# A gated DeltaNet layer step: the samples' gate column turned on VectorE and stored as rows, blocks of 8 spread through GpSimd's queue, the samples' substitution one block later

## The chip, the cores and the metric

The kernel runs on one core of a Trainium2 chip. The metric is the device time of one execution in microseconds (us). Before the change the median of three runs is 1664.96 us (1664.11 to 1667.59).

## The reference, cut to what matters

One decoder layer works on 256 prompt tokens and on 8 samples of 4 tokens each. One wide projection feeds a short gated convolution (A) and a gated DeltaNet mixer (B) of 8 heads; merge gates, an output projection, a layer norm, a feed-forward part and a second layer norm follow. The part that this document is about is the delta rule of mixer B:

```python
gcum = jnp.cumsum(gc, axis=-1)
diff = gcum[..., :, None] - gcum[..., None, :]
decay = jnp.where(causal, jnp.exp(jnp.where(causal, diff, 0.0)), 0.0)
M = jnp.where(strict, jnp.einsum('nbhid,nbhjd->nbhij', kb, kc) * decay, 0.0)
T = lax.linalg.triangular_solve(eye + M, eye, left_side=True, lower=True, unit_diagonal=True)
u = T @ (vc * bc)
w = T @ (kb * jnp.exp(gcum)[..., None])
```

For a pair of positions the decay is the difference of two running sums of the gate, so the kernel needs these sums both down the partitions (a column) and along the free axis (a row that every partition holds). The triangular matrix is inverted by forward substitution: the prompt's in blocks of 8 that are then merged to 16, 32 and 64, the samples' in blocks of 4.

## The kernel before, in words

All weights stream once from HBM in chunks of 512 KB (tile `raw`), which the text calls blocks, by their number. Float32 products are made of three matmuls, so each chunk is split: ScalarE copies it to a rounded high half (`hi`, L185), VectorE subtracts to make the low half (`lo`, L140, called from `split_lo`), and TensorE multiplies high by both halves of the activations (L217) and low by the high one (L219). A block has 24 such matmuls. The main loop (L1647 on) writes out the order by hand. In turn i it issues, in this order: the high split of block i + 3; one step of the side work; the low split of block i + 3; evacuations of finished accumulators that are due; the matmuls of block i; the load of block i + 7 on SP's queue. Each of the tiles `raw`, `hi` and `lo` has four buffers. So a load on SP waits until VectorE has made the low half that frees its buffer, and the splits are at most three blocks ahead of TensorE.

The side work is a Python generator: each `yield` ends the turn's step. It computes the gates (`gates`, L1019), then the delta rule for heads 0 to 3 (`gdn(0)`, called group 0) and 4 to 7 (group 1). Within each engine and each queue, instructions go in program order: a DMA on SP that waits for something holds every later weight load, and a VectorE instruction that waits holds the next low split.

What the change and the prediction's steps touch:

- L1083 to L1097: running sums by matmul; the prompt's sums are written to DRAM (`sums_d`) as rows from 16 partitions.
- L1113 to L1122: `s1` holds the samples' values per partition: column [.., 0, n] is the running sum of the gate, for the head groups n = 0, 1. L1121 writes each of the two columns to DRAM (`srow_d`), 128 single floats each.
- L1133, one turn later: SP reads them back as a row that is copied to all 128 partitions (`srow`); its reader is `sample()` (L1429), far on.
- L1212, one turn later again: SP reads the prompt's sums as rows into `gl`; VectorE's first use is E (L1234), three turns on.
- L1276 to L1283: VectorE makes the 8 x 8 diagonal blocks `n8`; SP writes them to DRAM (`eight_d`, L1279), and a turn later reads them back so that each partition holds its whole block (`X`, in tile `xt`, L1282). GpSimd's copies `move_sums(1)` stand between. Three turns on, VectorE starts the substitution (L1336 to L1344); its result goes to the matmuls of `pairs` (L1333).
- L1294: GpSimd's queue loads two of the group's four old states (L1146); later `spread_kq` on GpSimd (L1316); both are read by `states_of` (L1324).
- `sample()` is stepped from the same main loop after the side step. It writes 4 x 4 blocks to DRAM (L1439), reads them a turn later (L1441), moves k in quarters over two turns (`quarters`), then makes the substitution of 4 on VectorE (L1444 to L1450). A turn later its matmul follows (L1454).

Of the kernel before, what the change touches and what calls it, by code (L numbers as in the profile page):

```python
# [9 lines left out]
F32 = mybir.dt.float32  # L10
# [6 lines left out]
P = 128  # L17
# [85 lines left out]
def hybrid_kernel(ctx: ExitStack, tc: tile.TileContext, A):  # L103
# [3 lines left out]
    def pool(name, bufs=1, **kw):  # L107
        return ctx.enter_context(tc.tile_pool(name=name, bufs=bufs, **kw))

    cp = pool("cp")  # L110
# [5 lines left out]
    dp = pool("dp", space=bass.MemoryType.DRAM)  # L116
# [3 lines left out]
    def nm(s):  # L120
        counter[0] += 1
        return f"{s}{counter[0]}"

    def gtile():
        n = nm("g")
        return gp.tile([P, 512], F32, tag="g", name=n)
# [5 lines left out]
    def bmid(ap, n):  # L132
        sh = list(ap.shape)
        return ap.unsqueeze(1).to_broadcast([sh[0], n] + sh[1:])

    act, dve, pe, gps, sp = nc.scalar, nc.vector, nc.tensor, nc.gpsimd, nc.sync


    def tt(out, a, b, op):
        dve.tensor_tensor(out=out, in0=a, in1=b, op=op)  # L140
# [93 lines left out]
    def cst(n):  # L234
        a, b = CF_AT[n]
        if a >= NL:
            return ph["late"][:, a - NL:b - NL]
        return cf[:, a:b] if a < NE else cfe[:, a - NE:b - NE]
# [15 lines left out]
    epsc = cp.tile([P, 3], F32, name="epsc")  # L254
    hmr = cp.tile([P, P], F32R, name="hmr")
    sums_d = dp.tile([4, 2, 256], F32, name="sums_d")
    srow_d = dp.tile([2, P, 1], F32, name="srow_d")
    four_d = [dp.tile([32, 4, 4], F32, name=f"four_d{G}") for G in range(2)]
    eight_d = [dp.tile([16, 8, 64], F32, name=f"eight_d{G}") for G in range(2)]
    stBA = cp.tile([P, 32, 32], F32, name="stBA")  # L260
# [756 lines left out]
    G_ = {}  # L1017

    def gates(first):  # L1019
# [47 lines left out]
        tt(gm, bmid(g[:, 2, :], 8), bc(cst("bm3"), 8), MUL)  # L1067
        by_row = cp.tile([P, P], F32, name="by_row")
        gps.memset(by_row, 0.0)
        for r in range(2):  # L1070
            gps.tensor_copy(by_row[:, 8 * r:8 * r + 8].rearrange("p (n a b) -> p n a b", n=2, a=2),
                            g[:, 0:2, :].rearrange("p b (n r a) -> p r n a b", n=2, r=2)[:, r])
# [8 lines left out]
        q = gtile()  # L1081
# [29 lines left out]
        yield  # L1111
        next(first)
        s4 = cp.tile([P, 4, 8], F32, name="s4")  # L1113
        s1 = cp.tile([P, 4, 2], F32, name="s1")
        tt(s4[:, 0:2], q[:, 128:144].rearrange("p (q h) -> p q h", h=8), bmid(cst("sel"), 2), MUL)
        tt(s4[:, 2:4], sb, bmid(cst("sel"), 2), MUL)
        dve.tensor_reduce(out=s1.rearrange("p a b -> p (a b)"), in_=s4.rearrange("p q (g h) -> p (q g) h", h=4),
                          axis=mybir.AxisListType.X, op=ADD)
        sx = cp.tile([P, 4, 2], F32, name="sx")
        for n in range(2):  # L1120
            sp.dma_start(srow_d[n], s1[:, 0, n:n + 1])  # L1121
        act.activation(sx[:, 0:2, :], s1[:, 0:2, :], AF.Exp)  # L1122
        yield
        next(first)
# [4 lines left out]
                  egls=ge[:, 32:96].rearrange("p (b h) -> p b h", b=8),  # L1129
                  s_g=s1[:, 3, :], s_beta=s1[:, 2, :], s_eg=sx[:, 0, :], s_kd=sx[:, 1, :],  # L1130
                  s_neg=sx[:, 2, :], s_ngc=sx[:, 3, :])
        srow = cp.tile([P, 2, P], F32, name="srow")
        sp.dma_start(srow, srow_d.rearrange("n p o -> (o n) p").unsqueeze(0).to_broadcast([P, 2, P]))  # L1133
        G_["s_row"] = srow
        yield


    def gdn(G):
# [9 lines left out]
        def T(shape, tag):  # L1148
            return pl.tile(shape, F32, tag=tag, name=nm(tag))
# [8 lines left out]
        sqr = T([P, 1024], "vmh")  # L1158
# [34 lines left out]
        def move_k(copy, a, b):  # L1193
            for i in range(4):
                copy(kdec[64 * a + 32 * b:64 * a + 32 * b + 32, :, :, 32 * i:32 * i + 32],
                     ktv[32 * i:32 * i + 32, a, a, b])

        def move_sums(s):
            for b in range(2):
                for i in range(4):  # L1200
                    gps.tensor_copy(red4[64 * s + 32 * b:64 * s + 32 * b + 32, i].rearrange("p (c r) -> p c r", r=2),
                                    ptv[32 * i:32 * i + 32, 1 - s, b])
# [12 lines left out]
        total(3)  # L1215
        move_k(gps.tensor_copy, 0, 0)
        yield
        move_k(act.copy, 0, 1)
        yield
        sp2 = gtile()  # L1220
# [10 lines left out]
        X, Tm = xt[:, 0], xt[:, 1]  # L1231
# [35 lines left out]
        for u, q4, par, r in halves:  # L1267
# [8 lines left out]
        dve.tensor_reduce(out=n8, in_=Tm.rearrange("p q (b j) -> p q j b", b=8), axis=mybir.AxisListType.X, op=ADD)  # L1276
        tt(n8, n8, bmid(cst("i8u"), 8), MUL)
        tt(n8, n8, bmid(i8, 8), ADD)
        sp.dma_start(eight_d[G].rearrange("b k x -> (b k) x"), sqr[:, 0:64])  # L1279
        move_sums(1)  # L1280
        yield
        sp.dma_start(X.rearrange("p q c -> p (q c)"),  # L1282
                     eight_d[G].rearrange("b k x -> b (k x)").unsqueeze(1).to_broadcast([16, 8, 512]))  # L1283
        nb = X.rearrange("p q c -> p (q c)").rearrange("p (k q j) -> p q k j", k=8, q=8)
        kso = T([P, 2, P], "kso")
        kraw, ktok = (sqr[:, 512 + 256 * u:768 + 256 * u] for u in range(2))
# [121 lines left out]
        def quarters(out, src, side_):  # L1408

            act.copy(hl[:, 0], src)  # L1410
            tt(hl[:, 1], src, hl[:, 0], SUB)
            for hh in range(4):
                for w in range(4):
                    low = w // 2 if side_ == 0 else w % 2
                    d, r = out[32 * w:32 * w + 32, hh], hl[32 * hh:32 * hh + 32, low]
                    if side_ and w % 2:
                        act.copy(d, r)
                    else:
                        gps.tensor_copy(d, r)
                if hh % 2:  # L1420
                    yield

        def sample():

            sp1 = gtile()
            pe.matmul(sp1[:, 0:128], kst, kst, start=True, stop=True)
            pe.matmul(sp1[:, 128:256], kst, qst, start=True, stop=True)
            pe.transpose(sp1[:, 384:512], vfs.rearrange("p h b t -> p (h b t)"), ident)
            stt(Es, G_["s_row"][:, G], G_["s_ngc"][:, G:G + 1], cst("mbias4"), ADD, ADD)  # L1429
            act.activation(Es, Es, AF.Exp)  # L1430
            act.mul(vs, sp1[:, 384:512], snk)
            act.mul(kr, kr, sc[:, 0:1])
            stt(nMs, sp1[:, 0:128], sc[:, 2:3], Es, MUL, MUL)
            stt(aTs, sp1[:, 128:256], srk, Es, MUL, MUL)
            n4, u4, t4, r4 = (Ts[:, 4 * u:4 * u + (16 if u == 3 else 4)] for u in range(4))
            dve.tensor_reduce(out=n4, in_=nMs.rearrange("p (b j) -> p j b", j=4), axis=mybir.AxisListType.X, op=ADD)
            tt(n4, n4, cst("i4u"), MUL)
            tt(n4, n4, cst("i4"), ADD)
            sp.dma_start(four_d[G].rearrange("b k j -> (b k) j"), n4)  # L1439
            yield  # L1440
            sp.dma_start(r4, four_d[G].rearrange("b k j -> b (k j)").unsqueeze(1).to_broadcast([32, 4, 16]))  # L1441
            yield from quarters(kr3, kr, 0)
            rows4 = r4.rearrange("p (k j) -> p k j", k=4)
            dve.tensor_copy(u4, cst("i4"))  # L1444
            for j in range(1, 4):
                tt(t4[:, 0:j + 1], u4[:, 0:j + 1], rows4[:, 0:j + 1, j], MUL)
                dve.tensor_reduce(out=u4[:, j:j + 1], in_=t4[:, 0:j + 1], axis=mybir.AxisListType.X, op=ADD)
            tt(Us.rearrange("p (b j) -> p b j", j=4), u4.unsqueeze(1).to_broadcast([P, 32, 4]),
               cst("l4").rearrange("p (b j) -> p b j", j=4), MUL)
            stt(vs, kso[:, 0, :], G_["s_neg"][:, G:G + 1], vs, MUL, ADD)  # L1450
            act.mul(osm, kso[:, 1, :], G_["s_eg"][:, G:G + 1])
            yield
            pv_ = gtile()
            pe.matmul(pv_[:, 0:P], Us, vs, start=True, stop=True)  # L1454
            act.mul(vns, pv_[:, 0:P], sc[:, 1:2])
            v3 = pl.tile([P, 4, P], F32R, tag="U", name=nm("v3"))
            yield from quarters(v3, vns, 1)
            yield
            po = gtile()
            pe.matmul(po[:, 0:P], aTs, vns, start=True, stop=True)  # L1460
            tt(osm, osm, po[:, 0:P], ADD)
            done.append(1)
            vm = {}


            def spread(hh):
                if hh < 4:
                    vm[hh] = pl.tile([P, 8, P], F32R, tag=("vmh", "vml")[hh % 2], name=nm("vm"))
                    for b in range(8):
                        act.mul(vm[hh][:, b], v3[:, hh].bitcast(F32), cst("bmask")[:, b:b + 1])  # L1470

            spread(0)
            yield
            for hh in range(4):
                spread(hh + 1)
                if hh:
                    store(hh - 1)
                for j in range(2):
                    yield
                    pn = gtile()  # L1480
                    pe.matmul(pn, kr3[:, hh], vm[hh][:, 4 * j:4 * j + 4, :], start=True, stop=True)
                    for u in range(4):
                        b = 4 * j + u
                        stt(S0[:, hh, b], S0[:, hh, b], G_["egls"][:, b, 4 * G + hh:4 * G + hh + 1],
                            pn[:, u * P:u * P + P], MUL, ADD)
            yield
            store(3)
# [9 lines left out]
        o = T([P, 4, 2, P], "xt")  # L1497
# [103 lines left out]
    t, h0, l0 = raw.pop(0), his[0], los[0]  # L1601
# [170 lines left out]
```

## Time and profile before

| what | value |
|---|---|
| median of three runs | 1664.96 us |
| the profiled execution | 1664.45 us |
| its span, from first to last instruction | 1662.5 us |
| mean granted clock of TensorE | 0.999 |
| VectorE, ScalarE, GpSimd busy | 59%, 47%, 8% |
| mean DMA rate | 169 GB/s |

The profile is of one execution. Its span is shorter than the time by what lies around it, here 1.95 us. Rows of a timeline read: start, duration (us), engine, line, operation, out<-in, shapes, count, and in brackets the idle time of that engine just before and what ended it. SPq is a DMA that is issued on SP's queue; its duration is that of the issue, not of the transfer. In a list of waits the numbers are: us in total, times, longest. In a table by stretches of time they are: the stretch, its length, busy time and count of TensorE's matmuls, of its weight loads, of VectorE, ScalarE and GpSimd, then the granted clock, the DMA engines' mean busy share and GB/s.

### The profile page before, as it was taken

Reading aid. Unit: us, or ns where it says so; the run is one execution under the profiler, and the core shown is the slowest. Engines: PE = TensorE matmul, PEld = TensorE weight load, DVE = VectorE, ACT = ScalarE, POOL = GpSimd, SP = SyncE. Lnnn points to the kernel's source line nnn. Section 1 sums busy time; section 2 is a strip of 40 time slices with the busy share of each in tenths; the row PEclk is TensorE's granted clock in tenths of the full one; section 3 lists DMA queues with packets and bytes.
Section 4 is the critical chain, followed back from the end, with each engine's and each line's share of the span. In section 5 each row is a group of like instructions: output and inputs, shape, how many; then the busy total and the mean of one; then the engine's idle time right before and its main releaser. Section 6 shows DMA issues by size and latency. Waiting matters only on the chain.

```text
span 1662.5 us, 31404 instructions
## 1 busy us (share of the span) xinstructions
PE 1648.4 (99%) x13112; PEld 1633.2 (98%) x13112; DVE 977.4 (59%) x1305; ACT 782.6 (47%) x1224; POOL 134.9 (8%) x276
## 2 busy tenths in 40 slices
PE   9999999999999999999999999999999999999998
PEld 8989999999999999999999999999999999999998
DVE  6778677767544444457776666444444444444466
ACT  6776756457533333334444445443334433344344
POOL 1131315233000000000000000000000000000011
PEclk9999999999999999999999999999999999999999
DMA  8566466645755555555565555555555555555652
GB/s 263 167 165 183 138 186 194 195 117 152 213 165 166 165 163 169 167 166 164 159 219 165 164 168 162 167 165 166 167 164 165 165 167 167 165 165 165 181 162 100
DMA packets 275129, 281.40 MB, mean 169 GB/s; under 512 B 15108, under 2 KB 268601, under 8 KB 274725
## 3 DMA queue, kind: packets, MB, share of 16 engines
q1 hardware_dynamic: 271226, 267.31, 53.6%
q0 software_dynamic: 3616, 12.02, 2.5%
q8 instruction: 103, 1.69, 0.4%
q14 instruction: 40, 0.32, 0.1%
q10 hardware_dynamic: 144, 0.07, 0.0%
HBM read 271.79 MB, written 7.56 MB: 168 GB/s over the span
## 4 chain that ended last, share of the span: by engine, by line
PE 93%; DVE 2%; ACT 2%; DMA 2%; issue 1%; SPq 0%; ACTq 0%; DVEq 0%
PE acc L217 60%; PE acc L219 30%; DMA raw<-in_w_in_dram 1%; DVE lo L140 1%; PE acc L741 1%; ACT hi L185 1%; DMA srow_d<-s 1%; DVE w L143 0%; PE g L1333 0%; PE g L1503 0%; PE g L1523 0%; PE g L1526 0%; DMA xr<-in_x_prompt_dram 0%; PE g L1324 0%; PE g L1515 0%
## 5 line engine op out<-in xcount | busy, mean ns | idle before, releaser
L140 DVE TENSOR_TENSOR lo<-raw,hi 128x1024 fp32r<-128x1024 f32 (+1 forms) x503 | 606.8, 1210 | 577.5 <-ACT hi L185 576.5
L185 ACT CAST hi<-raw 128x1024 fp32r<-128x1024 f32 (+1 forms) x499 | 518.6, 1042 | 736.3 <-PE acc L217 643.0
L217 PE MATMUL acc<-xh,hi 128*128 128x288 f32 x1408 | 398.5, 299 | 0.5 <-ACT xh L948 0.4
L217 PE MATMUL acc<-xl,hi 128*128 128x288 f32 x1408 | 394.4, 295 | 0.0
L219 PE MATMUL acc<-xh,lo 128*128 128x288 f32 x1408 | 303.1, 296 | 5.4 <-DVE lo L140 5.3
L217 PE MATMUL acc<-dl,hi 128*128 128x288 f32 (+1 forms) x1024 | 287.7, 295 | 0.0
L217 PE MATMUL acc<-dh,hi 128*128 128x288 f32 (+1 forms) x1024 | 287.4, 295 | 0.0
L217 PE MATMUL acc<-hl,hi 128*128 128x288 f32 x992 | 277.8, 295 | 0.0
L217 PE MATMUL acc<-hh,hi 128*128 128x288 f32 x992 | 277.4, 294 | 0.0
L217 PEld LDWEIGHTS acc<-xh,hi 128*128 128x128 f32 x1408 | 265.0, 188 | 3.2 <-issue 1.6
L217 PEld LDWEIGHTS acc<-xl,hi 128*128 128x128 f32 x1408 | 264.8, 188 | 0.7
L219 PEld LDWEIGHTS acc<-xh,lo 128*128 128x128 f32 x1408 | 226.5, 188 | 6.9 <-DVE lo L140 6.9
L219 PE MATMUL acc<-dh,lo 128*128 128x288 f32 (+1 forms) x1024 | 219.7, 296 | 0.0
L219 PE MATMUL acc<-hh,lo 128*128 128x288 f32 x992 | 213.2, 296 | 0.0
L217 PEld LDWEIGHTS acc<-dh,hi 128*128 128x128 f32 x1024 | 193.3, 189 | 0.0
L217 PEld LDWEIGHTS acc<-dl,hi 128*128 128x128 f32 x1024 | 192.8, 188 | 0.0
L217 PEld LDWEIGHTS acc<-hh,hi 128*128 128x128 f32 x992 | 186.4, 188 | 0.4 <-issue 0.4
L217 PEld LDWEIGHTS acc<-hl,hi 128*128 128x128 f32 x992 | 186.1, 188 | 0.0
L219 PEld LDWEIGHTS acc<-dh,lo 128*128 128x128 f32 x1024 | 164.6, 188 | 0.0
L219 PEld LDWEIGHTS acc<-hh,lo 128*128 128x128 f32 x992 | 159.1, 188 | 0.0
L217 PE MATMUL acc<-mh,hi 128*128 128x288 f32 x256 | 71.9, 297 | 0.0
L217 PE MATMUL acc<-ml,hi 128*128 128x288 f32 x256 | 71.7, 295 | 0.0
(411 smaller groups left out, 1471.3 us busy)
## 6 DMA issues: line engine op xcount, KB each, us to landing
raw<-in_w_in_dram SPq DMA_DIRECT2D x175, 512.0 KB, 3.9
raw<-in_w_up_dram SPq DMA_DIRECT2D x128, 512.0 KB, 3.7
raw<-in_w_down_dram SPq DMA_DIRECT2D x128, 512.0 KB, 3.6
raw<-in_w_o_dram SPq DMA_DIRECT2D x32, 512.0 KB, 4.1
raw<-in_w_a_out_dram SPq DMA_DIRECT2D x16, 512.0 KB, 3.6
raw<-in_w_b_out_dram SPq DMA_DIRECT2D x16, 512.0 KB, 3.6
S<-in_state_gdn_dram POOLq DMA_DIRECT2D x8, 512.0 KB, 5.9
out_dram<-S POOLq DMA_DIRECT2D x8, 512.0 KB, 5.2
```

The lines of the kernel that those rows point to most:

```text
L140: dve.tensor_tensor(out=out, in0=a, in1=b, op=op)
L185: act.copy(his[i][:, k:k + step], raw[i][:, k:k + step])
L217: pe.matmul(o, h[:, k, c], x, start=st and x is xh_, stop=False)
L219: pe.matmul(o, l[:, k, c], xh_, start=False, stop=en)
L741: pe.matmul(out, x[:, kk, c], w[:, k, :], start=False, stop=stop)
```

## The change

The two columns are no longer written as single floats. `s1` becomes a part of a zeroed tile `st2`; one turn later VectorE transposes it in blocks of 32 x 32, so that each group of 32 partitions holds the sums of head groups 0 and 1 in its first two partitions as rows of 32 floats; SP writes four pieces of two such rows. The read-back moves from the gates into `gdn(0)`, three turns later than before, behind the read of `gl`. The write and the read of the blocks of 8 go from SP's to GpSimd's queue, and the read is issued in the turn of the write. In `sample()` one more `yield` stands before the substitution of 4; what follows in `sample()` comes a turn later too.

```diff
-    srow_d = dp.tile([2, P, 1], F32, name="srow_d")
+    srow_d = dp.tile([2, 4, 32], F32, name="srow_d")
...
         gps.memset(by_row, 0.0)
+        st2 = cp.tile([P, 2, 32], F32, name="st2")
+        gps.memset(st2, 0.0)
...
-        s1 = cp.tile([P, 4, 2], F32, name="s1")
+        s1 = st2[:, 0, 0:8].rearrange("p (a b) -> p a b", b=2)
...
         sx = cp.tile([P, 4, 2], F32, name="sx")
-        for n in range(2):
-            sp.dma_start(srow_d[n], s1[:, 0, n:n + 1])
         act.activation(sx[:, 0:2, :], s1[:, 0:2, :], AF.Exp)
         yield
...
-        srow = cp.tile([P, 2, P], F32, name="srow")
-        sp.dma_start(srow, srow_d.rearrange("n p o -> (o n) p").unsqueeze(0).to_broadcast([P, 2, P]))
-        G_["s_row"] = srow
+        dve.transpose(out=st2[:, 1], in_=st2[:, 0])
+        for n in range(4):
+            sp.dma_start(srow_d[:, n], st2[32 * n:32 * n + 2, 1])
+        G_["s_row"] = cp.tile([P, 2, P], F32, name="srow")
         yield
...
         move_k(gps.tensor_copy, 0, 0)
         yield
+        if G == 0:
+            sp.dma_start(G_["s_row"], srow_d.rearrange("n b t -> n (b t)").unsqueeze(0).to_broadcast([P, 2, P]))
         move_k(act.copy, 0, 1)
...
-        sp.dma_start(eight_d[G].rearrange("b k x -> (b k) x"), sqr[:, 0:64])
+        gps.dma_start(eight_d[G].rearrange("b k x -> (b k) x"), sqr[:, 0:64])
         move_sums(1)
-        yield
-        sp.dma_start(X.rearrange("p q c -> p (q c)"),
-                     eight_d[G].rearrange("b k x -> b (k x)").unsqueeze(1).to_broadcast([16, 8, 512]))
+        gps.dma_start(X.rearrange("p q c -> p (q c)"),
+                      eight_d[G].rearrange("b k x -> b (k x)").unsqueeze(1).to_broadcast([16, 8, 512]))
+        yield
...
             yield from quarters(kr3, kr, 0)
+            yield
             rows4 = r4.rearrange("p (k j) -> p k j", k=4)
```

## The prediction

> **What bounds the kernel now.** First the page: how busy TensorE is in the span.
>
> ```profile
> span 1662.5 us, 31404 instructions
> PE 1648.4 (99%) x13112; PEld 1633.2 (98%) x13112; DVE 977.4 (59%) x1305; ACT 782.6 (47%) x1224; POOL 134.9 (8%) x276
> ```
>
> TensorE works all the time; only 14.1 us of its span are idle, and only what an edit takes from this idle time can be won. Next the waits of TensorE, of which these three lie in the part that the diff touches (the others are at start and end):
>
> ```profile
> PE acc L219 <- DVE lo L140: 5.3, 4, 1.8
> PE g L1454 <- DVE b L143: 0.6, 1, 0.6
> PE g L1333 <- DVE U L1344: 0.2, 1, 0.2
> ```
>
> So 6.2 us is the most that can go. The timeline of TensorE between 107 and 131 us shows where the four waits of 5.3 us are:
>
> ```profile
> 108.79 0.53 PE L219 MATMUL acc<-xh,lo 128*128 128x288 f32 x2 [0.97 <-DVE lo L140]
> ...
> 113.89 0.53 PE L219 MATMUL acc<-xh,lo 128*128 128x288 f32 x2 [1.65 <-DVE lo L140]
> ...
> 125.77 0.54 PE L219 MATMUL acc<-xh,lo 128*128 128x288 f32 x2 [1.79 <-DVE lo L140]
> ...
> 130.15 0.53 PE L219 MATMUL acc<-xh,lo 128*128 128x288 f32 x2 [0.93 <-DVE lo L140]
> ```
>
> They add to 5.34 us. Each waits for a low half that VectorE made late. Why late: the chain of waits between 75 and 135 us names a DMA, then the timelines of SP, ScalarE and VectorE tell the rest.
>
> ```profile
> 84.05 9.11 DMA srow_d<-s
> ```
> ```profile
> 81.36 1.60 SPq L1096 DMA_DIRECT2D sums_d<-gq  x2
> ...
> 83.52 1.70 SPq L1121 DMA_DIRECT2D srow_d<-s  x2
> 85.76 0.38 SPq L175 DMA_DIRECT2D raw<-in_w_in_dram  x1
> 93.23 0.32 SPq L1133 DMA_DIRECT2D srow<-srow_d  x1
> 93.64 0.39 SPq L175 DMA_DIRECT2D raw<-in_w_in_dram  x1
> 94.21 0.55 SPq L1212 DMA_DIRECT2D gl<-sums_d  x1
> ```
> ```profile
> 96.79 1.05 ACT L185 CAST hi<-raw 128x1024 fp32r<-128x1024 f32 x1 [5.39 <-DMA raw<-in_w_in_dram]
> ...
> 107.56 1.04 ACT L185 CAST hi<-raw 128x1024 fp32r<-128x1024 f32 x1 [3.71 <-DMA raw<-in_w_in_dram]
> ```
> ```profile
> 86.01 0.70 DVE L1178 STREAM_TRANSPOSE S<-kq 128x512 f32<-128x512 f32 x1
> ...
> 86.89 1.21 DVE L140 TENSOR_TENSOR lo<-raw,hi 128x1024 fp32r<-128x1024 f32 x1
> ...
> 106.18 0.69 DVE L140 TENSOR_TENSOR E<-gl,gpt 128x512 f32<-128x512 f32 x1 [3.64 <-DMA gl<-sums_d]
> ...
> 128.87 1.22 DVE L140 TENSOR_TENSOR lo<-raw,hi 128x1024 fp32r<-128x1024 f32 x1
> ```
>
> Read it so. The two column writes (L1121) land at 93.16. SP holds their read (L1133) until 93.23, and block 28's weights (93.64) and the read of gl (94.21) stand behind it. Block 27's weights, issued at 85.76 ahead of that wait, still come only at 96.79, eleven us later. The DMA itself was slow; the busy times by stretch show it (last two columns: share of the DMA engines, GB/s):
>
> ```profile
> 82.00:86.00 4.00, 4.00 (x33) 4.00 (x32) 3.30 (x6) 3.94 (x14) 3.76 (x9) 1.00 1.05 317
> ...
> 90.00:94.00 4.00, 4.00 (x32) 4.00 (x32) 2.81 (x4) 1.40 (x3) 3.59 (x8) 1.00 0.59 37
> ...
> 106.00:110.00 4.00, 3.02 (x23) 2.79 (x22) 3.72 (x6) 2.41 (x3) 0.00 (x0) 1.00 0.16 44
> ```
>
> 317 GB/s before the column writes, 37 while they run, with engines busy: that is the cost of the first spot. From E at 106.18 VectorE then works with next to no gap to 130.09, and TensorE pays.
>
> **The change, part by part. The column as rows.** Removed: two DMAs of 128 single floats, and the 7 us in which SP holds. Added: a memset on GpSimd while it idles; a VectorE transpose of 128x32; four writes of two rows of 128 bytes. The transpose is not in the trace; by size it is a sixteenth of the 0.70 us one above, and it is no longer than that: 0.04 to 0.7 us, taken as 0.15, ahead of block 24's low half at 86.89. The writes wait for it, at about 87.1. Per write, SP takes between 0.34 (L1279 below) and 0.85 us (L1121, half of 1.70): 1.4 to 3.4 us for four; I take 0.34, since each has two rows against 128. Behind them stand block 28's weights (due after 88.1, when the low half frees their buffer) at about 88.9 instead of 93.64, and gl at 89.4 instead of 94.21, 91.4 at worst. The read of srow comes three blocks later, past gl and three weight loads; its writes have then had 4 us, and its consumer is far off in sample(). Block 27's weights are issued once and land before 91.40, when ScalarE fell idle, if the DMA keeps its 317 GB/s.
>
> How small pieces count is seen in the packets between 86 and 94 us:
>
> ```profile
> DMA packets 644, 0.36 MB, mean 45 GB/s; under 512 B 301, under 2 KB 643, under 8 KB 643
> ```
>
> 256 of the 301 small ones are the two columns; afterwards there are 8. [...]
>
> What is then late: gl. From issue to E it took 106.18 - 94.21 = 12.0 us. In group 1, with no column writes near, the same read took as long:
>
> ```profile
> 268.35 0.52 SPq L1212 DMA_DIRECT2D gl<-sums_d  x1
> ```
> ```profile
> 281.62 0.69 DVE L140 TENSOR_TENSOR E<-gl,gpt 128x512 f32<-128x512 f32 x1 [4.86 <-DMA gl<-sums_d]
> ```
>
> 13.3 us. After it, at 106 to 110, a DMA share of 0.16 is two to three engines of 16 working off a rest, so few engines carry gl, and the change does not touch that. I take 12.0: E at 101.4. The last stalled low half ends 130.09 - 106.18 = 23.9 us behind E, at 125.3. TensorE without stalls would want it at 130.15 - 5.34 = 124.8. So 0.5 us of stall is left, with 13.3 us and the slow writes (91.4) 3.8 us, with less than 11.4 us nothing. The same for the other input of that stretch: block 29's weights follow gl by 107.56 - 106.18 = 1.4 us, and its buffer is free when TensorE ends block 25. A block is 24 matmuls of 0.133 us:
>
> ```profile
> 420.00:1000.00 580.00, 580.00 (x4364) 580.00 (x4363) 334.81 (x361) 246.03 (x291) 1.64 (x3) 1.00 0.57 171
> ```
>
> 3.2 us; block 28 began 0.97 + 0.5 us before 108.79, so block 25 ended at 100.9. That is no later than gl. **Term: -5.3 + 0.5 = -4.8 us.**
>
> **Blocks of 8 through GpSimd.** SP loses two issues and their waits; the weights behind them leave earlier, worth nothing as no later load is waited for by TensorE. What was an SP round trip is now two GpSimd DMAs with a wait between; behind the wait stand two state loads (1 MB) and the spread of k and q, which matmuls read 40 us later in group 0:
>
> ```profile
> 118.53 1.76 POOL L1146 DMA_DIRECT2D S<-in_state_gdn_dram  x2 [22.30 <-ACT kdec L1195]
> ```
> ```profile
> 158.70 1.01 PE g L1324 x32
> ```
>
> Issued some ten us later they keep over 20; group 1 has the same order. What hangs on it is the substitution of 8. Group 1 has the least room:
>
> ```profile
> 299.05 0.34 SPq L1279 DMA_DIRECT2D eight_d<-vmh  x1
> ```
> ```profile
> 309.21 0.19 DVE L140 TENSOR_TENSOR vmh<-vmh,xt 128x16 f32<-128x16 f32 x1
> ```
>
> 10.2 us from issue to first use. If late there, TensorE pays at once, since L1333 already waits 0.2 us for the end of this chain. In group 0 four blocks lie between, 12.8 us. GpSimd's own DMAs and a copy, by line (issue ns, then landing us, min/median/max):
>
> ```profile
> L1582 POOL DMA_DIRECT2D out_dram<-st x16: 540/632/837, 260.7 to 390.4; - x16
> DMA to landing us min/median/max: 1.8/3.8/5.2
> ```
> ```profile
> L1146 POOL DMA_DIRECT2D S<-in_state_gdn_dram x8: 882/896/1048, 76.1 to 293.6; - x8
> DMA to landing us min/median/max: 4.8/5.9/8.2
> ```
> ```profile
> L1201 POOL COPY red<-part x32: 180/184/1115, 91.7 to 280.1; 32x8 f32<-32x8 f32 x32
> ```
>
> A write like the first (3.8) and a read no slower than the second (5.9): 9.7 us, inside 10.2; the eight sums copies (1.5 us) run beside the write. At worst 5.2 + 8.2 = 13.4: 3.2 us late in group 1, 0.6 in group 0. At best 6.6, and the 0.2 us of L1333 stays. **Term: 0**, for the median lies inside.
>
> **The samples' substitution a block later.** In group 1 the 0.6 us wait of L1454 is for this chain, which in its block stands behind VectorE's work on p1, from 356.99 on; the next block has only the product at 362.11 ahead of it:
>
> ```profile
> 356.99 1.46 DVE L143 SCALAR_TENSOR_TENSOR v<-g,gpt,v 64x128 f32<-64x128 f32 x4 [0.63 <-PE g L1503]
> ...
> 362.11 0.42 DVE L140 TENSOR_TENSOR v<-g,brk 128x256 f32<-128x256 f32 x1
> ```
>
> The chain and its matmul both move one block on, so what counts is the VectorE work ahead of the chain in its block: 0.42 us in place of at least 1.46. That is over 1.0 us less, more than the wait of 0.6, so the wait goes: **-0.6 us**. The sample ends a block later; group 1 starts after group 0's own end, and the merge is a few blocks off, so nothing waits.
>
> **Sum.** The profiled execution took 1664.45 us (span 1662.5, 1.95 around it), 0.5 below the median of 1664.96. 1664.45 - 4.8 - 0.6 = **1659.0 us**.
>
> **Rivals.** (1) gl stays late: slow issue, 13.3 us, or block 29 behind it. For it: 13.3 us in group 1; against: less is queued ahead. It leaves 1.8 to 3.8 us: about 1661.5. (2) The rows are as slow as the columns, or their wait moves to the new read, so the change does not do what it says. Then the 9 us lie one block later, on gl: about 1664. [...]
>
> **Chances.** Forecast 0.62, (1) 0.20, (2) 0.08, (3) 0.10. About 0.2% (3.3 us) is what a measurement can tell. Forecast and two thirds of (1) lie over 3.3 us below 1664.96: faster 0.75; the rest of (1) and (2): same 0.17; slower 0.08, part of (3) ending within 0.2%. Range: from no stall left and the 0.2 us gone too (1664.45 - 6.2 = 1658.2, and 0.4 for scatter) to the worst of (1), 1659 - 0.5 + 3.8 = 1662.3, and 0.7 for scatter and a late group 1: 1657.8 to 1663.
>
> **What would show it.** Right: no L1133-like wait over 2 us on SP; DMA above 250 GB/s from 86 to 90; block 27's split at about 91.4, E at 99 to 102; at most one short wait of L219 before 131; no wait at L1454. Wrong: E after 103 (rival 1), 37 GB/s again (2), VectorE idle on xt from GpSimd's queue and L1333 waiting over 1 us (3).

## The result and the profile after

| | before | after |
|---|---|---|
| median | 1664.93 us (1664.11 to 1667.59, 6 runs) | 1658.74 us (1658.17 to 1660.82, 6 runs) |
| the profiled execution | 1664.45 us | 1658.8 us |
| its span | 1662.5 us | 1656.9 us |

The ratio of the times is 0.9963, with a 95% interval of 0.995 to 0.9976. The changed kernel is about 6.2 us faster. The forecast of 1659.0 us is within 0.3 us of the measured median. That closeness is luck: one term of the sum was too small and two were too good, and they cancel. The code lines moved by a few: the writes of L1121 are now L1134 and their read of L1133 is L1220, L1212 is L1213, L1201 is L1202, L1279 and L1282 are L1282 and L1284, L1333 is L1336, L1341 is L1344, L1366 and L1367 are L1369 and L1370, L1454 is L1458.

The page of after, the two lines that answer to the first ones of before:

```profile
span 1656.9 us, 31407 instructions
PE 1646.9 (99%) x13112; PEld 1632.9 (99%) x13112; DVE 978.3 (59%) x1306; ACT 782.9 (47%) x1224; POOL 139.6 (8%) x281
```

TensorE has the same 13112 matmuls; 10.0 us of its span are idle instead of 14.1. The waits of TensorE in after, those in the part that changed:

```profile
PE g L1336 <- DVE U L1370: 1.5, 1, 1.5
...
PE g L1458 <- DVE b L143: 0.6, 1, 0.6
```

The four waits of L219 are gone. A wait of 1.5 us is new, and the 0.6 us of the samples' matmul is still there. The timeline of TensorE in after shows where both are:

```profile
148.50 0.75 PE L1336 MATMUL g<-U,gl 32*32 32x32 f32 x64 [1.54 <-DVE U L1370]
...
190.09 0.46 PE L1458 MATMUL g<-b 128*128 128x128 f32 x2 [0.62 <-DVE b L143]
```

Both lie in group 0. The 0.6 us of before were in group 1; those are gone, and a wait of the same length stands in group 0.

Now the start of the chain, SP in after:

```profile
86.85 1.18 SPq L1134 DMA_DIRECT2D srow_d<-st  x4
88.14 0.40 SPq L175 DMA_DIRECT2D raw<-in_w_in_dram  x1
88.63 0.56 SPq L1213 DMA_DIRECT2D gl<-sums_d  x1
```

Four row writes are issued in 1.18 us, block 28's weights leave at 88.14 instead of 93.64, and gl at 88.63 instead of 94.21. SP no longer waits for the writes to land. It now waits 2.8 us for the transpose, ahead of the four writes (L1134 for L1132 in its list of waits). That costs nothing here: block 28's weights, next on SP, were due only after 88.1, when their buffer came free.

ScalarE and VectorE in after, for the same pieces of work:

```profile
91.68 1.06 ACT L185 CAST hi<-raw 128x1024 fp32r<-128x1024 f32 x1 [0.33 <-PE acc L217]
...
100.36 1.05 ACT L185 CAST hi<-raw 128x1024 fp32r<-128x1024 f32 x1 [1.61 <-PE acc L217]
```
```profile
86.54 0.20 DVE L1132 STREAM_TRANSPOSE st<-st 128x32 f32<-128x32 f32 x1
...
98.56 0.69 DVE L140 TENSOR_TENSOR E<-gl,gpt 128x512 f32<-128x512 f32 x1 [1.12 <-DMA gl<-sums_d]
...
131.97 0.19 DVE L140 TENSOR_TENSOR vmh<-vmh,xt 128x16 f32<-128x16 f32 x1 [1.92 <-DMA xt<-eight_d]
```

Block 27 is split at 91.68 instead of 96.79 and block 29 at 100.36 instead of 107.56. Both now wait for TensorE, no longer for a DMA. E runs at 98.56 instead of 106.18. The last row is the new trouble: VectorE stands 1.92 us before it has the blocks of 8.

The DMA engines over the writes, after, in the first stretch and then by packets from 86 to 94 us:

```profile
86.00:90.00 4.00, 4.00 (x32) 4.00 (x31) 3.93 (x9) 3.48 (x8) 3.75 (x7) 1.00 0.55 158
```
```profile
DMA packets 1295, 1.37 MB, mean 171 GB/s; under 512 B 53, under 2 KB 1222, under 8 KB 1292
```

Between 86 and 94 us 1.37 MB move instead of 0.36 MB, and 53 packets under 512 B instead of 301.

GpSimd in after, group 0, then group 1:

```profile
121.99 0.57 POOL L1282 DMA_DIRECT2D eight_d<-vmh  x1 [26.61 <-DVE vmh L140]
122.60 4.62 POOL L1202 COPY red<-part 32x8 f32<-32x8 f32 x8
127.16 0.56 POOL L1284 DMA_DIRECT2D xt<-eight_d  x1
...
294.70 0.58 POOL L1282 DMA_DIRECT2D eight_d<-vmh  x1 [21.15 <-DVE vmh L140]
295.32 2.77 POOL L1202 COPY red<-part 32x8 f32<-32x8 f32 x8
298.02 0.56 POOL L1284 DMA_DIRECT2D xt<-eight_d  x1
```

The eight sums copies, which were priced at 1.5 us, take 4.62 us in group 0, and the read is issued only behind them.

To see what each of these is worth, I compared when the k-th matmul of the weight stream (L217 and L219, 24 to a block) starts in both traces, counted from the first one. Read at the blocks where the difference jumps:

| at block | after against before | what lies there |
|---|---|---|
| 2 | -0.4 us | arrival of the first inputs |
| 34 | -7.0 us | the four waits of L219 are gone: -6.7 |
| 40 | -5.4 us | the new wait of L1336: +1.6 |
| 70 | -4.6 us | group 0's sample: +0.9 |
| 100 | -5.8 us | group 1's sample wait is gone: -1.2 |
| end | -5.8 us | |

So in this pair of traces the change won 6.7 us with the rows, gave 1.6 back with the blocks of 8, and won 0.3 with the samples' later step; 0.4 lies at the start, which no edit touches.

### The profile page after: what moved, and what is told of

It is laid out like the page before. It is cut to its first block, busy times and chain, and to the rows that moved or that the text cites. A ratio compares the mean times of both kernels' runs of the same rounds, so it can differ in the third digit from the quotient of the medians.

```text
span 1656.9 us, 31407 instructions
## 1 busy us (share of the span) xinstructions
PE 1646.9 (99%) x13112; PEld 1632.9 (99%) x13112; DVE 978.3 (59%) x1306; ACT 782.9 (47%) x1224; POOL 139.6 (8%) x281
## 4 chain that ended last, share of the span: by engine, by line
PE 94%; DVE 3%; DMA 1%; ACT 1%; issue 0%; POOL 0%; SPq 0%; ACTq 0%; DVEq 0%; POOLq 0%
PE acc L217 60%; PE acc L219 30%; DVE lo L140 1%; PE acc L741 1%; DMA gl<-sums_d 1%; DVE w L143 1%; PE g L1507 0%; PE g L1527 0%; PE g L1530 0%; DMA xt<-eight_d 0%; POOL red L1202 0%; DMA xr<-in_x_prompt_dram 0%; PE g L1336 0%; PE g L1327 0%; PE g L1485 0%
## 5 line engine op out<-in xcount | busy, mean ns | idle before, releaser
L217 PE MATMUL acc<-xh,hi 128*128 128x288 f32 x1408 | 398.4, 298 | 0.5 <-ACT xh L948 0.4
L217 PE MATMUL acc<-xl,hi 128*128 128x288 f32 x1408 | 394.4, 295 | 0.0
L219 PE MATMUL acc<-xh,lo 128*128 128x288 f32 x1408 | 303.1, 296 | 0.0
L217 PE MATMUL acc<-dl,hi 128*128 128x288 f32 (+1 forms) x1024 | 287.7, 295 | 0.0
L217 PE MATMUL acc<-dh,hi 128*128 128x288 f32 (+1 forms) x1024 | 287.5, 295 | 0.0
L217 PE MATMUL acc<-hl,hi 128*128 128x288 f32 x992 | 277.8, 295 | 0.0
L217 PE MATMUL acc<-hh,hi 128*128 128x288 f32 x992 | 277.5, 294 | 0.0
L217 PEld LDWEIGHTS acc<-xh,hi 128*128 128x128 f32 x1408 | 265.0, 188 | 3.2 <-issue 1.4
L217 PEld LDWEIGHTS acc<-xl,hi 128*128 128x128 f32 x1408 | 264.9, 188 | 0.7
L219 PEld LDWEIGHTS acc<-xh,lo 128*128 128x128 f32 x1408 | 226.6, 188 | 0.2 <-DVE lo L140 0.2
L219 PE MATMUL acc<-dh,lo 128*128 128x288 f32 (+1 forms) x1024 | 219.9, 296 | 0.0
L219 PE MATMUL acc<-hh,lo 128*128 128x288 f32 x992 | 213.3, 296 | 0.0
L217 PEld LDWEIGHTS acc<-dh,hi 128*128 128x128 f32 x1024 | 193.3, 189 | 0.0
L217 PEld LDWEIGHTS acc<-dl,hi 128*128 128x128 f32 x1024 | 193.0, 188 | 0.0
L217 PEld LDWEIGHTS acc<-hh,hi 128*128 128x128 f32 x992 | 186.4, 188 | 0.4 <-issue 0.4
L217 PEld LDWEIGHTS acc<-hl,hi 128*128 128x128 f32 x992 | 186.3, 188 | 0.0
L219 PEld LDWEIGHTS acc<-dh,lo 128*128 128x128 f32 x1024 | 164.5, 188 | 0.0
L219 PEld LDWEIGHTS acc<-hh,lo 128*128 128x128 f32 x992 | 159.0, 188 | 0.0
L217 PE MATMUL acc<-mh,hi 128*128 128x288 f32 x256 | 71.9, 297 | 0.0
L217 PE MATMUL acc<-ml,hi 128*128 128x288 f32 x256 | 71.7, 295 | 0.0
```

Source lines behind the costliest of these rows:

```text
L217: pe.matmul(o, h[:, k, c], x, start=st and x is xh_, stop=False)
L219: pe.matmul(o, l[:, k, c], xh_, start=False, stop=en)
```

## The experiments

My theory after the result: all of the gain comes from the rows; the blocks of 8 come late because the read waits behind the sums copies; the sample's step moves its wait from one group to the other. Rivals: the states' loads crowd out the weights and so make the substitution late; and the holding of SP by the old read, not the slow column writes, was what cost 6.7 us. Eight kernels ran, each against the kernel before on the same chip: the first four on one chip, where before took 1663.64 us (15 runs), the last four on another, where it took 1665.57 us (21 runs). Each has 5 runs; the third, seventh and eighth have 11. The changed kernel itself did not run beside them, so they are compared with it (0.9963) by their ratio. An interval of the ratio is 1.5 to 2 us wide to each side; what a part of 1 to 2 us is worth is therefore read from the traces.

| kernel | median us | lowest to highest | ratio to before (95%) |
|---|---|---|---|
| rows alone | 1657.67 | 1656.66 to 1658.59 | 0.9963 (0.9951 to 0.9976) |
| after, blocks of 8 on SP | 1657.45 | 1656.46 to 1658.53 | 0.9961 (0.9949 to 0.9974) |
| after, sample as before | 1660.15 | 1658.95 to 1662.35 | 0.9977 (0.9968 to 0.9986) |
| after, read ahead of the copies | 1656.64 | 1656.26 to 1658.35 | 0.996 (0.9948 to 0.9973) |
| the same, later step in group 1 only | 1655.94 | 1655.59 to 1658.22 | 0.9945 (0.9932 to 0.9957) |
| after, states' loads first | 1659.35 | 1658.53 to 1662.56 | 0.9966 (0.9953 to 0.9978) |
| columns kept, the other two parts | 1667.71 | 1665.25 to 1671.74 | 1.0016 (1.0007 to 1.0025) |
| columns kept, only the read later | 1663.07 | 1661.72 to 1664.93 | 0.9987 (0.9978 to 0.9996) |

**1. The rows alone.** Against after, the other two parts are undone:

```diff
-        gps.dma_start(eight_d[G]..., sqr[:, 0:64])
+        sp.dma_start(eight_d[G]..., sqr[:, 0:64])
...
             yield from quarters(kr3, kr, 0)
-            yield
```

> The kernel before with the first part of the change alone: the gate columns turned on VectorE, written as rows, read back three turns later; blocks of 8 on SP's queue and the samples' substitution as before. Theory: all that is won comes from this part. The four waits of TensorE for low halves between 107 and 131 us go (worth 6.7 us by the shift of the matmuls between the two traces), there is no new wait at the second merge of group 0 (1.5 us after the change), and the 0.6 us wait of the samples' matmul in group 1 stays. Time 1657.3 to 1658.3 us, below the changed kernel's 1658.7. Rival: the move of the blocks of 8 off SP's queue is needed for it, as SP otherwise holds the weights behind it; then some low-half waits stay and the time is 1660 to 1662 us.

0.9963, the same ratio as the whole change. In the waits of TensorE neither L219 nor L1370 is left; the sample's wait is where it was before, in group 1:

```profile
PE g L959 <- DMA xr<-in_x_prompt_dram: 1.9, 1, 1.9
...
PE g L1457 <- DVE b L143: 0.6, 1, 0.6
```

Between blocks 2 and 34 the matmuls gain 6.7 us on before, and after that nothing. This one edit carries the whole gain. That it is better than the whole change, as expected from the 1.6 us, the times don't show. The first row is the wait for the first input at the start, which no edit touches; here it alone is over 1 us longer than in before.

**2. After, with the blocks of 8 back on SP.** Write and read go to SP again, with the read a turn later as before; the rest is after.

> The changed kernel with the second part undone: the blocks of 8 are written and read back on SP's queue, the read one turn after the write. Theory: GpSimd's queue brings the blocks late in group 0 (VectorE idle 1.9 us at 131.97, then no gap until the merge at 148.50, where TensorE waits 1.5 us); on SP they land by about 130, so this wait goes and the time falls by 1.0 to 1.6 us, to 1657.1 to 1657.7. Rival: the late weights (ScalarE idle 3.1 us at 137.52) or VectorE's own load make the wait at the merge; then it stays within 0.5 us of 1.5 and the time at 1658.5 or above.

1657.45 us, 0.9961. The 1.5 us wait of L1336 for L1370 is gone, and group 0's wait of 0.6 us stays. So the new wait belongs to the move of the blocks of 8. That the time lies in the expected range is no proof of it: before was 1.3 us quicker on this chip than beside the changed kernel, and the ratio is that of after within its interval.

**3. After, with the sample as before.**

```diff
             yield from quarters(kr3, kr, 0)
-            yield
```

> The changed kernel with the third part undone: the samples' substitution where it was. Theory: the third part wins 1.0 us in group 1 and loses 0.9 us in group 0, as the chain lands in each case in or out of the block in which VectorE works on p1; undone, the 0.6 us wait is in group 1 again and not in group 0, and the time is the same within 0.4 us: 1658.4 to 1659.1. Rival: the part is a gain by itself; then 1659.5 or more.

Slower than expected: 1660.15 us (0.9977). As expected, group 1 has its 0.6 us again and group 0 none. But the wait behind the blocks of 8 was 1.8 us, and TensorE ran slowly after it. The wait ended at 148.77. Two stretches of this kernel, with that wait and behind it:

```profile
145.69:149.10 3.41, 1.59 (x47) 1.36 (x48) 3.35 (x6) 1.74 (x3) 3.24 (x5) 1.00 0.05 9
149.10:152.51 3.41, 3.41 (x60) 3.35 (x47) 2.37 (x3) 2.52 (x8) 3.22 (x4) 0.50 0.85 261
```

The granted clock (third column from the right) falls to half. TensorE's timeline there:

```profile
150.29 0.44 PE L217 MATMUL acc<-xh,hi 128*128 128x288 f32 x1
150.53 0.44 PE L217 MATMUL acc<-xl,hi 128*128 128x288 f32 x1
```

Matmuls start 0.24 us apart instead of 0.13, for 3.4 us; by the starts of the matmuls that costs 1.3 us more. In after, with a wait of 1.54 us, the clock stays at 1.00. What made it fall here is not shown; the last section sets it beside other waits.

**4. After, with the read directly behind the write,** the sums copies after both:

```diff
         gps.dma_start(eight_d[G]..., sqr[:, 0:64])
-        move_sums(1)
         gps.dma_start(X..., eight_d[G]...)
+        move_sums(1)
```

> The changed kernel with GpSimd's read of the blocks of 8 issued directly behind their write, and the eight copies of sums behind both. Theory: after the change the read was issued at 127.16, 5.2 us after the write, because the eight copies between them took 4.6 us; the write itself lands in 1.7 to 2.7 us. So the read goes 2 to 3 us earlier, VectorE's 1.9 us wait at the substitution goes, the merge's 1.5 us wait with it, and the time falls by 1.0 to 1.6 us to 1657.1 to 1657.7. Rival: the merge waits for something else (late weights behind the two state loads), then the time stays at 1658.5 to 1659.

1656.64 us, 0.996: below the expected range, but on the quicker chip, and by the ratio not to be told from after. GpSimd and VectorE of this kernel:

```profile
121.13 0.57 POOL L1282 DMA_DIRECT2D eight_d<-vmh  x1 [26.64 <-DVE vmh L140]
123.16 0.56 POOL L1283 DMA_DIRECT2D xt<-eight_d  x1 [1.46 <-DMA eight_d<-vmh]
123.77 5.33 POOL L1202 COPY red<-part 32x8 f32<-32x8 f32 x8
```
```profile
129.19 0.19 DVE L140 TENSOR_TENSOR vmh<-vmh,xt 128x16 f32<-128x16 f32 x1
```

GpSimd waits 1.46 us for the write to land, issues the read 2.0 us behind the write instead of 5.2, and VectorE finds the blocks there. The wait of L1336 for L1370 is gone. GpSimd's queue as such was not slow; the copies between were. This rests on the waits in the traces of this experiment and the next; the ratio differs from that of after by only 0.0003.

**5. That, and the sample's later step only where it helps.** `if G == 1:` ahead of the added `yield`.

> The changed kernel with the read of the blocks of 8 directly behind their write (as in the run before) and the samples' substitution a block later in group 1 alone. Theory: the only waits of TensorE left inside the kernel are then the 0.2 us at the first merge of group 1; against the run with the read first, the samples' wait of 0.6 us in group 0 (0.9 us by the shift of the matmuls) goes. On a chip where the kernel before takes 1663.6 us it takes 1655.5 to 1656.3 us, about 7.5 us less than the kernel before. Rival: the chain of the samples in group 0 waits elsewhere when it comes a block earlier; then no gain over the run with the read first.

1655.94 us, 0.9945: the best of all. By the ratio that is 9.2 us under before (7.2 to 11.3), by the starts of the matmuls from block 2 on 7.8. The expected time was for a chip on which before takes 1663.6 us, and here it took 1665.57, so what it forecast is the 7.5 us. Of TensorE's waits in the part that changed only this one is left:

```profile
PE g L1336 <- DVE U L1347: 0.3, 1, 0.3
```

It beats before clearly. Its interval touches that of after, but it ran on one chip beside the next kernel, which is after with two loads moved and has the waits of after: 1655.59 to 1658.22 against 1658.53 to 1662.56 us, with no overlap.

**6. After, with the states' loads first.** The two loads of old states go ahead of the write of the blocks of 8, so that they no longer stand in the way of the weights:

```diff
+        states_in(2)
+        states_in(3)
         gps.dma_start(eight_d[G]..., sqr[:, 0:64])
...
-        states_in(2)
-        states_in(3)
```

> The changed kernel with the loads of the two later states put on GpSimd's queue ahead of the write of the blocks of 8, so that they go out before 118 us as in the kernel before. Theory (late read): the merge's wait of TensorE stays at 1.5 us (1.0 to 2.0), because the eight slow copies still stand between write and read; only the late weights at 137.5 (3.1 us of ScalarE's time) go. The time stays within 0.5 us of the changed kernel. Rival (weights crowded out by the 1 MB of states): the wait at the merge goes and the time falls by 1.5 us, as far as with the read first.

1659.35 us, 0.9966: no gain over after, as expected. In after ScalarE waited 3.08 us for weights while the states loaded; here it does not, and TensorE's wait is still there:

```profile
137.52 1.05 ACT L185 CAST hi<-raw 128x1024 fp32r<-128x1024 f32 x1 [3.08 <-DMA raw<-in_w_in_dram]
```
```profile
138.57 1.05 ACT L185 CAST hi<-raw 128x1024 fp32r<-128x1024 f32 x1 [0.97 <-PE acc L217]
```
```profile
148.90 0.75 PE L1336 MATMUL g<-U,gl 32*32 32x32 f32 x64 [1.82 <-DVE U L1370]
```

The first fence is after, the other two are this kernel. The late weights were not the cause; the rival falls.

**7. The columns kept, the two other parts made.** `srow_d`, `s1`, the two column writes and the early read as before; blocks of 8 on GpSimd and the added `yield` as in after.

> The kernel before with the second and third part alone: columns of single floats and the held read as before, the blocks of 8 on GpSimd's queue, the samples' substitution a block later. Theory: the four low-half waits before 131 us stay in whole (5.3 us of idle time), the two parts add the wait at the merge of group 0, about 1.5 to 2 us, as the blocks of 8 are then needed 7 us or more later but made as much later too; the samples' part moves its wait from group 1 to group 0. The time is 0 to 2 us above the kernel before. Rival: off SP's queue the blocks of 8 free the weights behind them, and the time falls by 1 us or more.

1667.71 us, 1.0016: slower than before, by some 2.1 us going by the medians. The waits of TensorE:

```profile
PE acc L219 <- DVE lo L140: 6.3, 4, 2.0
...
PE g L1333 <- DVE U L1367: 0.9, 1, 0.9
```

The four waits are back, and a shorter form of the new wait too (0.9 us). By the starts of the matmuls the new wait and the samples' step cost 0.7 us together. Another 1.1 us lies in the first of the four waits, before the blocks of 8 are written; why it is longer than in before is not shown. So the two parts win nothing without the rows, and cost a part of the 2.1 us.

**8. The columns kept, only their read later.** Before, with the read of `srow` moved three turns on, past gl; the column writes stay:

```diff
-        sp.dma_start(srow, srow_d.rearrange("n p o -> (o n) p")...)
...
+        if G == 0:
+            sp.dma_start(G_["s_row"], srow_d.rearrange("n p o -> (o n) p")...)
```

> The kernel before with one edit: the columns are still written as single floats, at their old place, but their read back stands three turns later, behind the read of gl and three weight loads, so SP does not hold the queue for it. Theory (the slow part is the writes themselves): the DMA still moves 30 to 60 GB/s from 87 to 93 us, block 27's weights still land after 94 us, and as gl and block 28's weights are issued 5 us earlier only a part of the waits goes: 1 to 3 us are won, out of the 6.7 of the rows. Rival (the held queue is what costs): without the hold nearly all is won, 5 us or more, as with the rows.

1663.07 us, 0.9987: 2.5 us by the medians, of the 6.7 (0.7 to 3.7 by the interval). SP no longer waits for the column, yet the DMA still crawls. TensorE's waits for low halves, SP, the packets between 86 and 94 us, ScalarE and VectorE of this kernel:

```profile
PE acc L219 <- DVE lo L140: 3.3, 2, 1.8
```
```profile
87.83 0.55 SPq L1210 DMA_DIRECT2D gl<-sums_d  x1
```
```profile
DMA packets 275, 0.26 MB, mean 33 GB/s; under 512 B 19, under 2 KB 275, under 8 KB 275
```
```profile
95.73 1.05 ACT L185 CAST hi<-raw 128x1024 fp32r<-128x1024 f32 x1 [5.19 <-DMA raw<-in_w_in_dram]
```
```profile
103.99 0.69 DVE L140 TENSOR_TENSOR E<-gl,gpt 128x512 f32<-128x512 f32 x1 [2.50 <-DMA gl<-sums_d]
```

gl is issued as early as in after (87.83), but takes 16.2 us to E instead of 9.9. Block 27's weights are nearly as late as in before. The packets of the floats start before 86 us here (286 small ones between 84 and 86), and the slow stretch goes on behind them. Two of the four waits are left, of 1.56 and 1.79 us; with 0.28 us more each (see below) they make 3.9 us. Behind the second the clock falls to half once more:

```profile
124.92:128.33 3.41, 3.41 (x17) 3.41 (x16) 3.31 (x10) 3.34 (x8) 0.00 (x0) 0.50 0.43 142
```

So this execution gained only 1.2 us on before by the starts of its matmuls, and would have gained some 2.8 (6.7 less 3.9) without that stretch. The holding of SP cost some 2.5 us, then, and the slow writes of single floats the larger part, about 4: they slow down what is under way beside them. One thing is not separated: the rows are also written a turn later than the columns were, so that block 27's weights are issued ahead of them, no longer behind. Columns at that later place were not run, so how much of the gain is the form of the writes and how much their place stays open; for gl, which is issued behind the writes in both kernels, it is the form.

## Why the prediction was right, point by point

**What bounds the kernel: right, with one misreading.** The four low halves were the cost, and the chain from the column writes over gl and E was the cause; 1 and 8 show it. "So 6.2 us is the most that can go" was wrong: the four waits alone gave 6.7. These waits cost more than the idle time that is shown. Compare TensorE at the first of them, before (the row of 108.79 stands between these two), and an undisturbed place of after:

```profile
107.52 0.29 PE L217 MATMUL acc<-xl,hi 128*128 128x288 f32 x1
...
109.16 0.29 PE L217 MATMUL acc<-xh,hi 128*128 128x288 f32 x1
```
```profile
104.01 0.29 PE L217 MATMUL acc<-xl,hi 128*128 128x288 f32 x1
104.14 0.42 PE L219 MATMUL acc<-xh,lo 128*128 128x288 f32 x2
104.40 0.30 PE L217 MATMUL acc<-xh,hi 128*128 128x288 f32 x1
```

Undisturbed, the steps are 0.13 and 0.26 us. In before they are 1.27 and 0.37. So 1.25 us were lost where the row shows 0.97 idle: a matmul's record is 0.29 us long while the next one normally starts after 0.13, and that overlap is lost too. Some 0.28 us more for each of four waits make 1.1 of the 1.4 us by which 6.7 exceeds 5.34. The rest is spread over small gaps.

**Column as rows: mechanism right, the term too small (-4.8, measured -6.7).** The transpose took 0.20 us (taken: 0.15), the writes about 0.26 us each on SP (taken: 0.34), block 28's weights left at 88.14 (88.9), gl at 88.63 (89.4), and block 27 was split at 91.68 (91.4). The step that failed was "I take 12.0: E at 101.4": gl took 98.56 - 88.63 = 9.9 us. That is under the 11.4 us named as the point below which no stall is left, and none was left. The price of a wait, above, did the rest. In group 1 the read still took 13.4 us (13.3 in before); why it took less in group 0 stays open. The share of 0.16 at 106 to 110 was no sign that few engines carry gl, since E at 106.18 shows that gl had landed by then. Two signs were wrong: SP waited 2.8 us ahead of the row writes, and "DMA above 250 GB/s from 86 to 90" was 158. The weights were on time all the same, at a busy share of 0.55: the loads that were issued had ended. So the 158 GB/s were no sign of a slow DMA here; little was queued.

**Blocks of 8 through GpSimd: wrong (0, measured +1.6).** Two steps failed. "The eight sums copies (1.5 us) run beside the write": they took 4.62 us, and since the read stands behind them on the same queue, they and not the write set its time. In before they had run at 91.74, right behind the first eight; in after they stand behind the write, which waits 26.61 us for VectorE, and so come beside two low splits. The DMAs themselves were quicker than priced: the read landed 4.7 us after its issue. The chain of waits of after shows both:

```profile
123.37 1.09 POOL red L1202
124.50 1.10 POOL red L1202
...
127.16 4.72 DMA xt<-eight_d
```

So the round trip came out at 131.97 - 121.99 = 10.0 us, close to the 9.7 forecast, by errors that cancel. The second failing step is the room: "In group 0 four blocks lie between, 12.8 us", and with it "Group 1 has the least room". It was counted in blocks of TensorE, not read. The rows of before show the write and the first use in group 0:

```profile
128.98 0.34 SPq L1279 DMA_DIRECT2D eight_d<-vmh  x1
```
```profile
137.31 0.19 DVE L140 TENSOR_TENSOR vmh<-vmh,xt 128x16 f32<-128x16 f32 x1
```

That is 8.3 us, less than group 1's 10.2 and less than the forecast trip of 9.7: by these rows the forecast would have had the blocks 1.4 us late. The stalls that the rows remove have no part in it. In after VectorE was ready for the blocks at 131.97 - 1.92 = 130.05, 8.1 us behind the write, and in experiment 7, which keeps the stalls, 8.1 us as well. In group 1 the same 10.0 us (first use 304.69) fit into the room and no wait came up. Experiment 4 bears it out: there the blocks were used 8.1 us after the write was issued, and the wait is gone.

**The samples' substitution: wrong in its sum (-0.6, measured -0.3).** Group 1's wait went, as argued, and was worth 1.2 us. Group 0 (+0.9) was not considered, and there the step put the chain into a block in which it stands behind VectorE's work on p1. VectorE of after in group 0:

```profile
185.88 1.46 DVE L143 SCALAR_TENSOR_TENSOR v<-g,gpt,v 64x128 f32<-64x128 f32 x4 [0.32 <-PE g L1507]
...
188.04 0.15 DVE L1448 COPY b<-cf 128x4 f32<-128x4 f32 x1
```

In before the chain started there at 184.99, with nothing of p1 ahead of it in its block.

**Rivals.** (1) fell: E came at 98.56, not after 103. (2) fell: 53 small packets, and the weights came on time. (3), the slower one with its 0.10, fell, though its signs came in group 0: VectorE was idle on xt for 1.92 us and L1336 waited 1.54 us, worth 1.6 us, and the kernel was faster all the same. GpSimd's DMA issues, which a larger price would need, are stretched in no run: those of the blocks of 8 kept 0.56 to 0.58 us beside VectorE. The copies did not keep theirs (1.10 us instead of 0.18), and through program order the copies held the read. The row of L1201 in the prediction, 180/184/1115 ns, has the slow copies already; the eight sums copies were priced by its median. In experiment 7 this part and the samples' step, without the rows, leave the kernel slower than before.

## What to carry to other kernels

Read the room of a round trip from the rows of each pass, from the write to the first use; a count of turns times the length of a block gave 12.8 us where the rows show 8.3. On a queue that computes and issues DMAs, put the second half of a round trip directly behind the first, since what stands between holds it: here eight copies held it for 4.62 us, where eight times their median of 0.184 us made 1.5. Where one edit of a schedule serves several passes of a loop, look at each pass; the same step can remove a wait in one and make it in another.

## What the runs showed of the hardware

**Single floats and the transfers beside them.** Where 256 floats were written one by one, all transfers together ran at 33 to 45 GB/s for 8 us, though the writes carry 1 KB; over the 8 rows of 128 bytes, in the same 8 us, it was 171 GB/s, and no weights came late (blocks 27 and 29 were split at 91.68 and 100.36, where ScalarE waited for TensorE). The read of gl took 16.2 us beside the single floats and 9.9 us beside the rows. What in the writes slows the rest is not shown.

**GpSimd's copies beside VectorE.** The eight copies of 32x8 floats took 1.74 us where VectorE ran no low split (after, 271.81) and 4.62, 2.77 and 5.33 us here; single ones 1.10 us instead of 0.18. In group 0 of after VectorE was running low splits meanwhile, among them these two:

```profile
123.19 2.36 DVE L140 TENSOR_TENSOR lo<-raw,hi 128x1024 fp32r<-128x1024 f32 x2
```

The two slow copies, from 123.37 to 125.60, run as long as these two low splits, 123.19 to 125.55, and 1.10 us is about one of them (1.22 us). GpSimd's DMA issues stayed at 0.56 to 0.58 us. Why the copies stretch and the issues do not is not shown.

**The clock after a wait.** A wait of 1.81 us (experiment 3) and one of 1.79 us (experiment 8) were followed by a granted clock of 0.50 for 3.41 us (149.10 to 152.51 and 124.92 to 128.33, in the rows of these experiments). After waits as long it did not fall: one of 1.82 us in experiment 6, which ended at 148.90, one of 1.79 us in before, which ended at 125.77, and one of 2.03 us in experiment 7. The first two fences are experiment 6 and before, in stretches of 2 us (the granted clock is the third column from the right); the third is TensorE in experiment 7:

```profile
147.00:149.00 2.00, 0.18 (x12) 0.10 (x15) 1.94 (x4) 0.89 (x1) 1.92 (x3) 1.00 0.00 1
149.00:151.00 2.00, 2.00 (x74) 1.96 (x74) 2.00 (x2) 1.21 (x4) 1.92 (x3) 1.00 0.86 269
```
```profile
125.00:127.00 2.00, 1.23 (x9) 1.24 (x10) 1.93 (x4) 0.00 (x0) 0.00 (x0) 1.00 0.60 162
127.00:129.00 2.00, 2.00 (x17) 1.99 (x15) 1.93 (x5) 1.64 (x4) 0.00 (x0) 1.00 0.80 251
```
```profile
110.39 0.53 PE L219 MATMUL acc<-xh,lo 128*128 128x288 f32 x2 [2.03 <-DVE lo L140]
110.76 0.29 PE L217 MATMUL acc<-xh,hi 128*128 128x288 f32 x1
110.89 0.29 PE L217 MATMUL acc<-xl,hi 128*128 128x288 f32 x1
```

The clock stays at 1.00 in the first two, and in the third the matmuls behind the wait start 0.13 us apart, not 0.24 as in experiment 3. So the length of the wait alone does not decide. What does is not shown: no run shifted a wait to try it, and how many of the timed runs of experiments 3 and 8 have the slow stretch stays open, since each has one trace.

**The start scatters.** In the ten traces the wait of TensorE for the first input is 0.2 to 1.9 us, whatever the edit, and what follows moves with it. Differences between experiments that are smaller than that were therefore read from the waits inside, not from the times.
